# Reordering the first block of a two-branch mixer kernel: when x, u^T's parts and q's scale are made

## The chip, the cores and the metric

One core of a Trainium2 chip runs the whole program. The metric is the device time of one execution, in microseconds (us). The engines are TensorE (PE, its weight loads PEld), VectorE (DVE), ScalarE (ACT), GpSimd (POOL) and the DMA queue that SyncE (SP) issues. Each engine works through its own list of instructions in order.

## The reference, cut to what matters

```python
def reference(x, norm_g, w_in, ...):            # x: 4096 frames x 1024
    u = rms_norm(h, norm_g[layer])
    p = u @ w_in[layer]                          # 1024 x 4616
    (sb_q, sb_k, sb_v, sb_z, m_q, m_k, m_v, m_o, m_z, m_i, m_f) = jnp.split(p, split_at, axis=-1)
    sb = stick_breaking_attention(sb_heads(sb_q), sb_heads(sb_k), sb_heads(sb_v))
    sb_out = sb * jax.nn.silu(sb_z)
    ...
    mix = jnp.concatenate([sb_out, ml_out], axis=-1)
    h = h + mix @ w_out[layer]
    return rms_norm(h, final_norm_g)
```

The change lies in the first block of 512 frames, before any attention: x is normalised to u, u is transposed, and the first projections (v, then q and k) are made from it.

## The kernel before, in words

The frames are worked in blocks of 512 (four tiles p of 128 frames). Each block takes a row of "quanta": a quantum is one product of the transposed u of the block with 128 columns of weights, 24 matmuls of 128x512 (`t_quantum`, L486): for each of eight slices k of the model dimension three passes, high part of the weight times high part of u, high times low, low times high. Weights and u are split into two 16-bit parts each: the high part is a copy by ACT, the low part the difference, by DVE or POOL.

The first block has to make all of this before its first quantum. For each tile p: `x_in(p)` loads 128 rows of x (SP); `u_stats(p)` squares and sums them on ACT (L398) and forms the root on POOL (L400, L401); `u_scale(p)` multiplies them on DVE (L405); `u_first(p)` transposes them on PE (L1389) and copies the two halves out of PSUM, one by DVE (L1393) and one by ACT (L1391), into an fp32 tile; `v_mm(p)` is v's product in fp32 from that tile (L1406, called here the p-th fp32 product, from 0); `v_fin(p)` writes v's two parts (L583, L584) and the gates (L588) with v's scale. `u_parts(p, engine)` makes the 16-bit parts of u^T (ACT copy and subtraction, both at L1397 and L1398) and stores them to DRAM for the later sweeps (`scr_u`, L476).

A weight (`Prep`) is handled in three steps. `top` finds the largest absolute value (two reductions L279, then L282, L284, L286 on DVE). `scale` turns it into a scale by one PE transpose (L290) and five small DVE instructions (L292 to L297; the last writes `wgs`). `split` multiplies each of the two raw pieces by the scale (L307), takes the high part by ACT (L302) and the low part by subtraction (L303). The raw pieces of q (pair 0) lie in tiles named ATh, those of k in ATl, of the second q in bP, of the second k in sA. The DVE list of v's scale ends with L1421.

The order of all that is written out by hand at the end of `main_pass`. Things that belong to a later quantum are registered with `at(g, phase, ...)` and issued by `run(g, phase)`: the first q is quantum 2, then k, the second q, the second k. For the second block (tiles 4 to 7), x is loaded, scaled and transposed in the quanta of the first (`u_T`, L469 to L471); from tile 8 on x is loaded by `x_grid`, four transfers of small pieces (L424), and its squares are summed by L432. The pool of x tiles, `st`, has six buffers. `sb_alloc` and `sb_zero` clear the k tiles `kl` and `kh` of the attention.

The diff's lines of the kernel, with the callers:

Of the kernel before, what the change touches and what calls it, by code (L numbers as in the profile page):

```python
# [200 lines left out]
def main_pass(ctx, tc, x2, norm_g, win, win_k, b_ig, b_fg, conv_w, conv_b, hn_g, wout_k, fn_g,  # L201
              out2, scr_u, scr_m, scr_w, scr_M, scr_E, flag):
    nc = tc.nc
    V, G, A, PE, SP = nc.vector, nc.gpsimd, nc.scalar, nc.tensor, nc.sync
# [22 lines left out]
    def at(g, phase=None, fn=None):  # L227
        if phase is None:
            g, phase = g
        acts[g, phase].append(fn)  # L230

    def run(g, phase):
        for fn in acts.pop((g, phase), []):
            fn()
# [30 lines left out]
    class Prep:  # L265
# [31 lines left out]
            V.tensor_scalar(out=self.gs, in0=CT[:, 64:72], scalar1=SC[:, self.sid, 0:1], scalar2=None, op0=ALU.mult)  # L297

        def split(self, engines):
            for (r, k0, h, l), e in zip(self.pieces, engines):  # L300
                self.mult(r, k0, e)
                A.activation(out=h, in_=r, func=AF.Copy)  # L302
                e.tensor_tensor(out=l, in0=r, in1=h, op=ALU.subtract)  # L303

# [82 lines left out]
    def x_in(p):  # L387
        t = us[p] = stage()
        SP.dma_start(out=t, in_=x2[p * 128:(p + 1) * 128, :])
# [3 lines left out]
    def u_stats(p):  # L393
        t = us[p]
        ss = rnorm[p] = sm.tile([128, 1], F32, tag="ss", name="ss")
        ss2 = sm.tile([128, 2], F32, tag="ss2", name="ss2")
        for half in range(2):
            A.activation(out=ph_tile("yx", [128, 512]), in_=t[:, half * 512:(half + 1) * 512], func=AF.Square, scale=DM ** -0.5 / SU,  # L398
                         accum_out=ss2[:, half:half + 1])
        G.tensor_scalar(out=ss, in0=ss2[:, 0:1], scalar1=ss2[:, 1:2], scalar2=EPS / SU ** 2, op0=ALU.add, op1=ALU.add)  # L400
        G.tensor_tensor(out=ss, in0=ss, in1=mhalf[:, 0:1], op=ALU.pow)  # L401
# [106 lines left out]
    kl = [None, None]  # L508
# [4 lines left out]
    def sb_alloc():  # L513
        nonlocal qs, kh
        qs = wp.tile([128, 4, 512], F16, tag="wnb", name="qs")
        kh = wp.tile([128, 4, 640], F16, tag="kh", name="kh")
        for i in range(2):
            kl[i] = ph_tile(f"kl{i}", [128, 2, 640], F16)
            V.memset(kl[i][64:128, 0, :], 0.0)
            V.memset(kl[i][0:64, 1, :], 0.0)  # L520

    def sb_zero(pair):
        V.memset(kh[:, 2 * pair:2 * pair + 2, 0:128], 0.0)
        V.memset(kl[pair][:, :, 0:128], 0.0)

    def sb_scales(s):

# [434 lines left out]
    for p in range(4, 128 + 4):  # L962
        Q, i = divmod(p, 4)
        gq = blk_g(Q - 1)
        if p < NT:
            if Q == 1:
                at(gq + i, "pre", lambda p=p: x_in(p))
                at(gq + 1 + i, "pre", lambda p=p: (u_stats(p), u_scale(p)))
                gu = gq + i + 3
                at(gu, "pre", lambda p=p: u_T(p, 0))  # L970
                at(gu, "mid", lambda p=p: u_T(p, 1))
                at(gu, "post", lambda p=p: u_store(p))
            else:
                gu = gq + 2 * i
                at(gu - 7, "pre", lambda p=p: x_grid(p))
                at(gu - 5, "mid", lambda p=p: grid_stats(p))
                at(gu - 3, "pre", lambda p=p: grid_sum(p))
                at(gu - 2, "mid", lambda p=p: grid_scale(p))
                at(gu - 1, "pre", lambda p=p: grid_T(p))
                at(gu + 1, "pre", lambda p=p: u_split(p, V if p % 2 else G))  # L980
        elif p < 128:
            at(gq + 1 + i, "pre", lambda p=p: u_load(p))
# [365 lines left out]
    with tc.manual_schedule():  # L1348
# [27 lines left out]
        def wfill(name, tag):  # L1376
            return w_first(WTS[0, name], WT[0, name], sb_cols(0)[name], tag)
# [3 lines left out]
        def u_first(p):  # L1381
            t, u = us.pop(p), u_of(p)
            u32[p] = wt_tile().rearrange("p a k t -> p (a k t)").bitcast(F32).rearrange("p (k t) -> p k t", k=KT)
            for half in range(2):
                ks = slice(4 * half, 4 * half + 4)
                ps = ps_tile("zu", [128, 4, 128])
                for k in range(4):
                    c = (4 * half + k) * 128
                    PE.transpose(ps[:, k, :], t[:, c:c + 128], idf)  # L1389
                if half:  # L1390
                    A.activation(out=u32[p][:, ks, :], in_=ps, func=AF.Copy)  # L1391
                else:
                    V.tensor_copy(out=u32[p][:, ks, :], in_=ps)  # L1393

        def u_parts(p, eng):
            u = u_of(p)
            A.activation(out=u[:, 0], in_=u32[p], func=AF.Copy)  # L1397
            eng.tensor_tensor(out=u[:, 1], in0=u32[p], in1=u[:, 0], op=ALU.subtract)  # L1398
            u_store(p)
# [3 lines left out]
        def v_mm(p, tag):  # L1403
            ps = vps[p] = ps_tile(tag, [128, 512])
            for k in range(KT):
                PE.matmul(ps[:, 0:264], u32[p][:, k, :], vraw[:, k, :], start=(k == 0), stop=(k == KT - 1))  # L1406

        def v_fin(p):
            fin_v(0, p, vps.pop(p), SV[:, 0:1], 1.0 / SU)

        def v_top():
            m = sm.tile([128, 24], F32, tag="wm", name="wm")
            V.tensor_reduce(out=m[:, 0:KT], in_=vraw, op=ALU.max, axis=AX.X, apply_absolute_value=True)
            mx = sm.tile([128, 1], F32, tag="wx", name="wx")
            V.tensor_reduce(out=mx, in_=m[:, 0:KT], op=ALU.max, axis=AX.X)
            pv.mb = sm.tile([128, 128], F32, tag="wmb", name="wmb")
            V.tensor_copy(out=pv.mb, in_=mx[:, 0:1].to_broadcast([128, 128]))

        def v_scale():
            pv.scale()  # L1420
            V.tensor_scalar(out=SV, in0=SC[:, WNS[0], 0:1], scalar1=S_QKV, scalar2=None, op0=ALU.mult)  # L1421
# [13 lines left out]
        x_in(2)  # L1435
        x_in(3)
        qk = [wfill("q0", "ATh"), wfill("k0", "ATl"), wfill("q1", "bP"), wfill("k1", "sA")]
        u_stats(1)
        u_scale(1)
        v_mm(0, "pj")  # L1440
        u_stats(2)
        u_first(1)
        u_scale(2)
        v_top()
        v_mm(1, "pj")
        u_stats(3)
        u_first(2)
        u_scale(3)
        v_scale()
        v_mm(2, "o")  # L1450
        v_fin(0)
        u_first(3)
        qk[0].top()
        v_fin(1)
        u_parts(0, G)
        u_parts(1, G)
        run(0, "pre")
        v_mm(3, "o")
        run(0, "mid")
        run(0, "post")  # L1460
        qk[0].scale()
        qk[0].split([V, V])
        v_fin(2)
        u_parts(2, V)
        u_parts(3, G)
        qk[1].top()
        v_fin(3)
        run(1, "pre")
        run(1, "mid")
        run(1, "post")  # L1470
        sb_alloc()
        sb_zero(0)
        sb_zero(1)
        SP.dma_start(out=crow[0:32, 1, :], in_=conv_w[0].rearrange("t (g p) -> (t g) p", p=128))
        SP.dma_start(out=crow[32:40, 1, :], in_=conv_b[0].rearrange("(g p) -> g p", p=128))
        SP.dma_start(out=crow[0:4, 2, :], in_=hn_g[0].rearrange("(g p) -> g p", p=128))
# [112 lines left out]
```

## Time and profile before

| what | value |
|---|---|
| median of three runs | 2234.07 us (2233.28 to 2237.25) |
| the profiled execution | 2233.29 us, its span 2231.4 us |
| busy share of the span | PE 97%, DVE 66%, ACT 47%, POOL 43% |
| mean granted clock of PE | 0.989 of full speed |

The profiled execution spends 1.9 us outside its span. PE is busy nearly all the time after the first 140 us; the idle time that it has lies mostly ahead of that, where tiles, weights and scales of the first block are being made. A row of the timeline gives the start, the duration, the engine, the line, the instruction with its output and inputs, and in square brackets how long the engine stood idle before it and what released it.

### The profile page before, as it was taken

To read this page: it belongs to the slowest core of one execution; us is meant where nothing else is said; L and a number is where in the kernel's file an instruction comes from. 1 tells how busy PE (TensorE), PEld (TensorE's weight loads), DVE (VectorE), ACT (ScalarE), POOL (GpSimd) and SP (SyncE) were. 2 spreads that over 40 slices of the span, in tenths; PEclk is the share of its full clock that TensorE was granted. 3 is DMA by queue.
4 is the path that set the end of the run, shared out by engine and by line. 5 is a ranking of instruction groups with operands and counts; after the bars stand their busy time and mean duration, and the time that the engine had idled before them with its cause. 6 is when DMAs were issued, how large, how long until landed. Compare 5 with 4: busy or idle time off the path is not lost.

```text
span 2231.4 us, 36361 instructions
## 1 busy us (share of the span) xinstructions
PE 2156.6 (97%) x13731; PEld 1374.2 (62%) x13731; DVE 1474.8 (66%) x2886; ACT 1055.5 (47%) x1875; POOL 950.7 (43%) x1296
## 2 busy tenths in 40 slices
PE   6789999999999999999999999999999999999998
PEld 4456665666666666567666667766666666644443
DVE  5777777756777777755555555655555645788885
ACT  3566666555666666543322233333344322545443
POOL 2477777664555555521111011310333210577763
PEclk8899999999999999999999999999999999999999
DMA  6444444221222112222222213333322321555552
GB/s 184 96 80 99 99 98 100 72 72 57 66 74 76 63 63 72 72 85 46 69 76 76 68 61 81 105 113 95 91 71 82 89 75 56 166 175 174 175 178 92
DMA packets 230240, 208.68 MB, mean 94 GB/s; under 512 B 109492, under 2 KB 185320, under 8 KB 230056
## 3 DMA queue, kind: packets, MB, share of 16 engines
q1 hardware_dynamic: 230040, 206.27, 32.3%
q8 instruction: 110, 1.80, 0.3%
q14 instruction: 74, 0.61, 0.1%
q10 hardware_dynamic: 16, 0.00, 0.0%
HBM read 148.43 MB, written 53.61 MB: 91 GB/s over the span
## 4 chain that ended last, share of the span: by engine, by line
PE 80%; DVE 9%; POOL 4%; issue 3%; DMA 2%; ACT 1%; SPq 0%; DVEq 0%; POOLq 0%; ACTq 0%
PE ps_pj L486 34%; PE ps_pj L498 22%; PE ps_pj L1252 7%; PE ps_o L1252 3%; PE ps_at L628 2%; PE ps_zu L1252 2%; PE ps_o L644 2%; DVE zml L455 2%; DMA st<-in_x_dram 1%; PE ps_zu L834 1%; PE ps_zu L877 1%; PE ps_zu L878 1%; PE ps_zu L597 1%; PE ps_zu L596 1%; DVE qs L564 1%
## 5 line engine op out<-in xcount | busy, mean ns | idle before, releaser
L486 PE MATMUL ps_pj<-U,wT 128*128 128x512 f16 x4608 | 1046.4, 382 | 13.9 <-ACT U L1397 7.7
L486 PEld LDWEIGHTS <-wT 128*128 128x128 f16 x4608 | 452.1, 98 | 512.9 <-issue 14.6
L498 PEld LDWEIGHTS <-U 128*128 128x128 f16 x4512 | 441.1, 98 | 58.0 <-DVE kl L576 1.9
L498 PE MATMUL ps_pj<-wna,U 128*128 128x256 f16 (+1 forms) x2976 | 345.0, 273 | 1.9 <-DVE kl L576 1.6
L611 DVE TENSOR_TENSOR_SCAN bP<-bP,D 128x512 f32<-128x512 f32 x128 | 165.4, 1292 | 106.2 <-POOL bP L603 105.5
L1252 PEld LDWEIGHTS <-U 128*128 128x128 f16 x1344 | 131.6, 99 | 155.5 <-issue 1.3
L612 POOL TENSOR_TENSOR sA<-sA,bP 128x510 f32<-128x510 f32 x128 | 141.8, 1108 | 180.3 <-DVE bP L611 176.7
L890 POOL TENSOR_SCALAR rs<-mv 128x4 f32<-128x4 f32 x32 | 7.7, 240 | 453.3 <-DVE kl L784 395.5
L498 PE MATMUL ps_pj<-wnb,U 128*128 128x256 f16 x1536 | 178.1, 273 | 0.0
L785 ACT ACTIVATE kl<-ps_pj,SC 128x512 f32<-128x512 f32 x64 | 44.0, 688 | 232.8 <-PE ps_pj L486 190.6
L836 DVE TENSOR_TENSOR bP<-ps_zu,bP 128x512 f32<-128x512 f32 x32 | 22.1, 692 | 175.2 <-PE ps_at L835 174.2
L821 POOL TENSOR_SCALAR_AFFINE_SELECT bP<-bP 128x512 f32<-128x512 f32 x32 | 24.7, 771 | 255.8 <-DVE bP L820 225.8
L789 DVE SCALAR_TENSOR_TENSOR z<-kl,CT,z 128x512 f32<-128x512 f32 x144 | 115.1, 799 | 20.8 <-ACT z L786 16.0
L1252 PE MATMUL ps_pj<-wT,U 128*128 128x512 f16 x576 | 127.4, 379 | 1.2 <-DVE st L1257 1.2
L1263 ACT ACTIVATE kl<-st 128x512 f32<-128x512 f32 x64 | 40.4, 632 | 167.5 <-DVE st L1257 89.5
L798 ACT ACTIVATE v<-ps_pj,SC 128x256 f32<-128x256 f32 x64 | 30.4, 475 | 156.9 <-PE ps_pj L498 156.3
L633 DVE SCALAR_TENSOR_TENSOR ATl<-ps_at,ATh 128x512 f16<-128x512 f32 (+1 forms) x128 | 87.6, 685 | 16.7 <-ACT ATh L632 14.8
L1244 POOL TENSOR_TENSOR U<-sA,U 128x512 f16<-128x512 f32 x56 | 76.2, 1383 | 49.2 <-ACT U L1240 49.2
L547 ACT ACTIVATE zml<-ps_pj,SC 128x512 f32<-128x512 f32 x32 | 22.0, 688 | 151.1 <-DMA scr_m<-zml 137.5
L644 PE MATMUL ps_o<-ATl,v 128*128 128x256 f16 (+1 forms) x312 | 72.1, 252 | 20.0 <-DVE ATl L633 16.8
L600 ACT ACTIVATE bP<-ps_zu,SX 128x512 f32<-128x512 f32 x128 | 87.8, 686 | 3.6 <-issue 2.0
L601 ACT ACTIVATE sA<-ps_zu,SX 128x512 f32<-128x512 f32 x128 | 88.4, 690 | 0.0
(298 smaller groups left out, 3873.1 us busy)
## 6 DMA issues: line engine op xcount, KB each, us to landing
U<-scr_u SPq DMA_DIRECT2D x96, 512.0 KB
st<-in_x_dram SPq DMA_DIRECT2D x40, 512.0 KB
scr_u<-U SPq DMA_DIRECT2D x32, 512.0 KB
out_dram<-st SPq DMA_DIRECT2D x31, 512.0 KB
st<-in_w_in_dram SPq DMA_DIRECT2D x28, 512.0 KB
st<-in_x_dram SPq DMA_DIRECT2D x96, 128.0 KB
scr_m<-z SPq DMA_DIRECT2D x32, 256.0 KB
bP<-scr_M SPq DMA_DIRECT2D x32, 256.0 KB
```

The source lines that it names most:

```text
L455: V.tensor_scalar(out=z[:, :, b, :], in0=t[:, :, 2 * h + b, :], scalar1=r4[:, 2 * h + b:2 * h + b + 1], scalar2=None, op0=ALU.mult)
L486: PE.matmul(p3, wt[:, a, k, :], u[:, :, b, k, :], start=(k == 0 and i == 0), stop=(k == KT - 1 and i == 2))
L498: PE.matmul(ps[:, c0:c0 + n], u[:, a, k, :], w[:, b, k, 0:n], start=first and j == 0, stop=last and j == len(order) - 1)
L600: A.activation(out=b, in_=z, func=AF.Sigmoid, scale=SX[:, s, pair, 1:2])
L601: A.activation(out=sg, in_=z, func=AF.Sigmoid, scale=SX[:, s, pair, 0:1])
L611: V.tensor_tensor_scan(out=bf, data0=bf, data1=D1[:, ::-1], initial=1.0, op0=ALU.mult, op1=ALU.max)
L612: G.tensor_tensor(out=sg[:, :, 0:255], in0=sg[:, :, 0:255], in1=b[:, :, 1:256], op=ALU.mult)
L633: V.scalar_tensor_tensor(out=l[:, i:, :], in0=ps[:, i:, :], scalar=S_A, in1=h[:, i:, :], op0=ALU.mult, op1=ALU.subtract)
L644: PE.matmul(o[:, q0:q0 + 128 * n], vt[p][:, head, :], t, start=first, stop=False, skip_group_check=True)
L789: V.scalar_tensor_tensor(out=y, in0=raw[:, t:t + 512], scalar=CT[:, 8 * t + grp:8 * t + grp + 1], in1=y, op0=ALU.mult, op1=ALU.add)
L1244: (V if o in (0, 2, 6) else G).tensor_tensor(out=mo[p][:, o, 1], in0=mt[p][o], in1=mo[p][:, o, 0], op=ALU.subtract)
L1252: PE.matmul(ps, a[:, l, k, :], r[:, k, :], start=first and k == 0 and i == 0, stop=last and k == 3 and i == 2, skip_group_check=True)
```

## The change

The change moves calls in the hand-written order and moves eight clears from one engine to another. Nothing is computed differently.

- `split` becomes "multiply both pieces, then make both pairs of parts" (`parts`), and for the first q the three steps are issued apart: `top` behind the scaling of tile 2, `scale` directly behind v's scale, the two multiplications behind `u_parts(2)` and ahead of the last transposes of u, `parts` behind the last fp32 product.
- `u_parts(0)`, `u_parts(1)`, `u_parts(2)` stand behind the copies of their own tile or nearly so, all three subtractions on POOL; `u_parts(3)` goes to DVE. Before, tiles 0, 1 and 3 were POOL's and tile 2 was DVE's, all after the last copies.
- The loads of x for tiles 4 and 5 are issued directly behind the first weights; tiles 6 and 7 move up by one quantum.
- `v_top` stands ahead of the copies of tile 1, `v_fin(0)` and `v_fin(1)` behind the copies of tile 3.
- The clears of `kl` and `kh` go from DVE, between the scalings of tiles 4 and 5, to POOL, ahead of the root of tile 3.

```diff
         def split(self, engines):
-            for (r, k0, h, l), e in zip(self.pieces, engines):
+            for (r, k0, _, _), e in zip(self.pieces, engines):
                 self.mult(r, k0, e)
+            self.parts(engines)
+
+        def parts(self, engines):
+            for (r, _, h, l), e in zip(self.pieces, engines):
                 A.activation(out=h, in_=r, func=AF.Copy)
                 e.tensor_tensor(out=l, in0=r, in1=h, op=ALU.subtract)
...
-            V.memset(kl[i][64:128, 0, :], 0.0)
-            V.memset(kl[i][0:64, 1, :], 0.0)
-
-    def sb_zero(pair):
-        V.memset(kh[:, 2 * pair:2 * pair + 2, 0:128], 0.0)
-        V.memset(kl[pair][:, :, 0:128], 0.0)
+            G.memset(kl[i][64:128, 0, :], 0.0)
+            G.memset(kl[i][0:64, 1, :], 0.0)
+
+    def sb_zero(pair, e=V):
+        e.memset(kh[:, 2 * pair:2 * pair + 2, 0:128], 0.0)
+        e.memset(kl[pair][:, :, 0:128], 0.0)
...
-                at(gq + i, "pre", lambda p=p: x_in(p))
+                at(gq + max(i - 1, 0), "pre", lambda p=p: x_in(p))
...
         qk = [wfill("q0", "ATh"), wfill("k0", "ATl"), wfill("q1", "bP"), wfill("k1", "sA")]
+        run(0, "pre")
         u_stats(1)
         u_scale(1)
         v_mm(0, "pj")
         u_stats(2)
+        sb_alloc()
+        sb_zero(0, G)
+        sb_zero(1, G)
+        v_top()
         u_first(1)
         u_scale(2)
-        v_top()
+        qk[0].top()
         v_mm(1, "pj")
         u_stats(3)
+        u_parts(0, G)
         u_first(2)
         u_scale(3)
         v_scale()
+        qk[0].scale()
+        u_parts(1, G)
+        u_parts(2, G)
+        for r, k0, _, _ in qk[0].pieces:
+            qk[0].mult(r, k0, V)
         v_mm(2, "o")
+        u_first(3)
         v_fin(0)
-        u_first(3)
-        qk[0].top()
         v_fin(1)
-        u_parts(0, G)
-        u_parts(1, G)
-        run(0, "pre")
         v_mm(3, "o")
+        qk[0].parts([V, V])
+        u_parts(3, V)
+        v_fin(2)
+        qk[1].top()
         run(0, "mid")
         run(0, "post")
-        qk[0].scale()
-        qk[0].split([V, V])
-        v_fin(2)
-        u_parts(2, V)
-        u_parts(3, G)
-        qk[1].top()
         v_fin(3)
         run(1, "pre")
         run(1, "mid")
         run(1, "post")
-        sb_alloc()
-        sb_zero(0)
-        sb_zero(1)
```

The lists of three engines show the moves. First DVE before, from q's scale on (wx, SC and wgs are the scale, ATh the raw q, wT its parts, U the parts of u^T):

```order
L292 TENSOR_REDUCE wx<-ps_zu 128x1
L293 TENSOR_SCALAR wx<-wx 128x1
L294 RECIPROCAL SC<-wx 128x1
L295 TENSOR_SCALAR SC<-wx 128x1
L297 TENSOR_SCALAR wgs<-CT,SC 128x8
L307 TENSOR_TENSOR ATh<-ATh,wgs 128x512
L303 TENSOR_TENSOR wT<-ATh,wT 128x512
L307 TENSOR_TENSOR ATh<-ATh,wgs 128x512
L303 TENSOR_TENSOR wT<-ATh,wT 128x512
L584 SCALAR_TENSOR_TENSOR v<-ps_o,SV,v 128x4x64
L588 TENSOR_SCALAR GR<-ps_o 128x8
L1398 TENSOR_TENSOR U<-wT,U 128x1024
```

And DVE of the change, from the same instruction on (here L311 is the multiplication, L307 the subtraction, L1397 the copy of u^T, L588 and L592 are v's parts and gates):

```order
L292 TENSOR_REDUCE wx<-ps_zu 128x1
L293 TENSOR_SCALAR wx<-wx 128x1
L294 RECIPROCAL SC<-wx 128x1
L295 TENSOR_SCALAR SC<-wx 128x1
L297 TENSOR_SCALAR wgs<-CT,SC 128x8
L311 TENSOR_TENSOR ATh<-ATh,wgs 128x512 x2
L1397 COPY wT<-ps_zu 128x512
L588 SCALAR_TENSOR_TENSOR v<-ps_pj,SV,v 128x4x64
L592 TENSOR_SCALAR GR<-ps_pj 128x8
L588 SCALAR_TENSOR_TENSOR v<-ps_pj,SV,v 128x4x64
L592 TENSOR_SCALAR GR<-ps_pj 128x8
L307 TENSOR_TENSOR wT<-ATh,wT 128x512 x2
```

Before, the last copy of u^T and v's first two ends stood above the first of these rows; now q's scale and both of its multiplications stand ahead of the copy that the last fp32 product reads.

POOL before, from the root of tile 3 on (ss is the root):

```order
L400 TENSOR_SCALAR ss<-ss_254 128x1
L401 TENSOR_TENSOR ss<-ss,mhalf 128x1
L1398 TENSOR_TENSOR U<-wT,U 128x1024 x3
L400 TENSOR_SCALAR ss<-ss_378 128x1
L401 TENSOR_TENSOR ss<-ss,mhalf 128x1
```

And POOL of the change, from the first clear to the same place:

```order
L523 MEMSET kl_230 64x640
L524 MEMSET kl_230 64x640
L523 MEMSET kl_233 64x640
L524 MEMSET kl_233 64x640
L527 MEMSET kh 128x2x128
L528 MEMSET kl_230 128x2x128
L527 MEMSET kh 128x2x128
L528 MEMSET kl_233 128x2x128
L404 TENSOR_SCALAR ss<-ss_278 128x1
L405 TENSOR_TENSOR ss<-ss,mhalf 128x1
L1402 TENSOR_TENSOR U<-wT,U 128x1024 x3
```

The eight clears stand ahead of tile 3's root; the three subtractions stay in the same place of POOL's list, now for tiles 0, 1 and 2.

SP's queue before, from the last of the first weights on (scr_u is the store of u^T's parts):

```order
L361 DMA sA<-in_w_in_dram 128x4x128 x2
L476 DMA scr_u<-U 128x2048 x2
L389 DMA st<-in_x_dram 128x1024
L476 DMA scr_u<-U 128x2048 x2
L389 DMA st<-in_x_dram 128x1024
L424 DMA st<-in_x_dram 32x32x32 x4
```

And SP's queue of the change from the same place:

```order
L365 DMA sA<-in_w_in_dram 128x4x128 x2
L393 DMA st<-in_x_dram 128x1024 x2
L480 DMA scr_u<-U 128x2048 x4
L393 DMA st<-in_x_dram 128x1024
L428 DMA st<-in_x_dram 32x32x32 x4
```

The loads of tiles 4 and 5 no longer stand behind stores that wait for POOL's and DVE's subtractions; the load of tile 6 and the four small-piece transfers of tile 8 now stand behind all four stores.

## Rows read from the trace of the kernel before

**Rows 1.** Windows of the span: busy time by engine, PE clock, DMA share, GB/s.

```profile
20.00:30.00 10.00, 9.41 (x50) 7.83 (x49) 5.70 (x19) 3.93 (x6) 1.49 (x1) 1.00 0.01 2
30.00:40.00 10.00, 1.35 (x5) 0.55 (x5) 7.52 (x15) 5.11 (x10) 4.26 (x3) 0.72 0.48 177
...
60.00:70.00 10.00, 4.01 (x17) 1.89 (x16) 7.48 (x18) 5.46 (x15) 3.90 (x6) 0.75 0.46 102
```

**Rows 2.** Timeline of PE from 25 to 73 us.

```profile
26.83 3.83 PE L1406 MATMUL ps_o<-vraw,wT 128*128 128x264 f32 x16 [0.35 <-DVE wT L1393]
...
40.73 4.44 PE L486 MATMUL ps_pj<-U,wT 128*128 128x512 f16 x11 [1.71 <-DVE wm L282]
...
45.11 2.75 PE L486 MATMUL ps_pj<-U,wT 128*128 128x512 f16 x12
...
52.86 5.30 PE L486 MATMUL ps_pj<-U,wT 128*128 128x512 f16 x12 [4.56 <-ACT wT L302]
```

**Rows 3.** Chain of waits from 28 to 62 us: start, duration, what.

```profile
31.53 1.22 DVE wgs L297
...
38.45 2.23 POOL U L1398
...
41.08 6.05 DMA st<-in_x_dram
...
47.24 0.73 ACT yx L398 x2
...
49.81 0.75 DVE st L405
...
51.45 0.70 DVE ATl L307
```

**Rows 4.** Timeline of DVE in the first 60 us.

```profile
15.99 0.69 DVE L1393 COPY wT<-ps_zu 128x512 f32<-128x512 f32 x1 [3.00 <-PE ps_zu L1389]
...
17.26 2.34 DVE L1413 TENSOR_REDUCE wm<-vraw 128x8 f32<-128x2112 f32 x1
...
23.01 0.23 DVE L297 TENSOR_SCALAR wgs<-CT,SC 128x8 f32<-128x8 f32 x1
...
26.08 0.69 DVE L1393 COPY wT<-ps_zu 128x512 f32<-128x512 f32 x1 [1.69 <-PE ps_zu L1389]
...
54.83 0.69 DVE L303 TENSOR_TENSOR wT<-ATl,wT 128x512 f16<-128x512 f32 x1 [0.70 <-ACT wT L302]
```

**Rows 5.** Timeline of ACT from 16 to 50 us.

```profile
21.47 0.60 ACT L1391 ACTIVATE wT<-ps_zu 128x512 f32<-128x512 f32 x1 [3.08 <-PE ps_zu L1389]
...
27.37 2.00 ACT L1397 ACTIVATE U<-wT 128x1024 f16<-128x1024 f32 x2
```

**Rows 6.** Timeline of POOL in the first 45 us.

```profile
1.36 0.53 POOL L1365 MEMSET D<- 128x512 f32 x1
...
18.49 0.30 POOL L400 TENSOR_SCALAR ss<-ss 128x1 f32<-128x1 f32 x1 [4.69 <-ACT yx L398]
...
28.51 4.21 POOL L1398 TENSOR_TENSOR U<-wT,U 128x1024 f16<-128x1024 f32 x2 [9.07 <-ACT U L1397]
```

**Rows 7.** Timeline of DVE and POOL from 127.5 to 135 us.

```profile
128.07 5.92 DVE L455 TENSOR_SCALAR zml<-st,r 128x256 f32<-128x256 f32 x4
...
129.55 4.29 POOL L1497 TENSOR_TENSOR wna<-vraw,wna 128x2112 f16<-128x2112 f32 x1
```

**Rows 8.** Timeline of SP's queue and ACT: small-piece loads of x and their readers.

```profile
41.60 5.42 SPq L424 DMA_DIRECT2D st<-in_x_dram  x4
...
59.24 0.41 ACT L432 ACTIVATE yx<-st 128x256 f32<-128x256 f32 x1
...
122.65 3.17 SPq L424 DMA_DIRECT2D st<-in_x_dram  x4
...
128.90 0.42 ACT L432 ACTIVATE yx<-st 128x256 f32<-128x256 f32 x1 [0.85 <-DMA st<-in_x_dram]
```

**Rows 9.** Waits of PE over the whole span: total us, times, longest.

```profile
PE ps_o L644 <- DVE ATl L633: 16.8, 12, 6.0
```

## Prediction

> **What bounds the kernel now.** I read the windows first, to see where PE is short of work. In the first block it is: between 30 and 40 us it is busy 1.35 of 10 us, between 60 and 70 us 4.01 [rows 1]. The timeline of PE shows what those holes are. q's quantum runs from its second matmul at 40.73, k's starts at 52.86 after 4.56 us of idle [rows 2]. Both holes are waits for DVE and ACT, so the next view is the chain of waits. Read it downwards: q's `wgs` at 31.53, the last of u^T's subtractions at 38.45 on POOL, then a load of x issued at 41.08 and landed 6.05 us later, its squares on ACT at 47.24, its scaling on DVE at 49.81, and behind that scaling, in DVE's list, k's multiplication at 51.45 [rows 3]. So k's weights wait for a load of x that k does not need, and that load waited in SP's queue behind stores of u^T that waited for POOL. From 51.45 on the chain goes on through DVE, ACT, POOL and PE; no transfer that is issued earlier comes into it, so what is gained at 51.45 should reach the end, unless the shift changes who collides with whom.
>
> I therefore follow one instruction, k's first multiplication (51.45 before), and then what its parts hold up, the multiplication of the second q.
>
> **Part 1: the loads of tiles 4 and 5.** They now stand behind the first weights. Between 20 and 30 us the DMA engines do nothing (share 0.01) [rows 1], and tile 5's load took 6.05 us even behind the stores [rows 3]; so both land well before 30 us, and ACT comes to them only after 33 (part 4). The 6.05 us leave the path. What ends the wait next is ACT's own list.
>
> **Part 2: `v_top` and the clears.** DVE stood idle 3.00 us ahead of the copy at 15.99; `v_top`, whose reduction takes 2.34 us, moves into that hole, and q's `top`, which is shorter, takes its old place at 17.26 [rows 4]. Both cost nothing there. The clears go to POOL, into its 4.69 us of idle ahead of 18.49, when tile 3's squares are ready. A POOL clear of 512 elements took 0.53 us; four of 640 and four of 256 come to about 4 us by that row (an estimate), which just fits [rows 6]. No row has a POOL clear beside DVE work: one DVE copy (`wmb`) or scaling could wait for one clear, so 0 to 0.7 us; I take 0, since the copies that PE waits for read PSUM.
>
> The Trainium skill, page "SBUF — State Buffer", section "Who interferes with whom", says that a GpSimd instruction that only writes SBUF holds up a DVE instruction in a two-port mode, but not one with two SBUF inputs. By it the clears could delay `wmb` and one scaling by the bound above, and nothing else; no run here shows it yet.
>
> **Part 3: u^T's parts and q's scale meet on one pair of ports.** ACT makes the high parts of tiles 1 and 2 directly behind the copy at 21.47, about 1.05 us each; a POOL subtraction starts 1.1 us after its ACT copy starts and takes 2.1 us [rows 5, 6]. So POOL subtracts from 23.1 to 25.2 and from 25.2 to 27.4. DVE ends v's scale as before (`wgs` at 23.01 [rows 4]) and comes with q's `wgs` at about 24.0. There I must choose. Before, this very instruction took 1.22 us instead of 0.23, ending when POOL's subtraction of 28.51 plus 4.21 ended [rows 3, 4, 6]: it was blocked. So in the change it waits until 25.2. Then come q's two multiplications, while POOL's next subtraction is already waiting. The nearest rows for that are from a later stage: four scalings of 256 elements on DVE took 5.92 us together [rows 7], though one of 1024 elements takes 0.75 [rows 3]; POOL's instruction of 129.55, which came while the third ran, went ahead of the fourth and held it to the end [rows 7]. So the turn goes to who waited first, and the multiplications start at 27.4 and end at 28.7 (0.69 each, overlapping a little). Only behind them stands the copy that the last fp32 product needs: 28.6 instead of 26.08 [rows 4].
>
> The same section of the Trainium skill says that the pair is an exclusive lock and that issue order decides who blocks; it speaks against this change, since it puts POOL's long instructions beside DVE's multiplications. By it the sum is the one below; without a lock it would be the first rival's.
>
> From there: the last fp32 product starts 0.75 us after its copy and takes 3.83 us [rows 2, 4], so 29.4 to 33.2. Meanwhile DVE does v's first two ends, q's two subtractions and tile 3's subtraction: by 0.69 us for 512 elements [rows 4] I estimate 0.5, 0.5, 0.7, 0.7 and 1.2 us, done by 33. q's quantum starts at 33.2 rather than 40.73, and if the clock stays up it takes twice 2.75 us, not 4.44 and 2.75 [rows 2]: end 38.7.
>
> **Part 4: to k's first multiplication.** ACT's list behind v's last end (33.2 to 33.6) holds the squares of tile 4, from 33.6, and of tile 5, from 35.1 (1.46 us for a tile, twice 0.73). From squares to scaling took 49.81 − 47.24 = 2.57 us, from scaling to k's multiplication 51.45 − 49.81 = 1.64 us [rows 3]. So 35.1 + 2.57 + 1.64 = 39.3 instead of 51.45: 12.1 us earlier. The clears, had they stayed on DVE, would lie on this stretch; now nothing does.
>
> **Part 5: both multiplications first.** For k's two pieces on DVE the old order took 54.83 + 0.69 − 51.45 = 4.07 us, with DVE waiting for ACT 0.70 us twice [rows 3, 4]. In the new order the second multiplication fills the first such wait and the second ACT copy runs under the first subtraction: about 1.35 us for the two multiplications, which overlap a little, and 1.3 for the two subtractions, 2.65 us: 1.4 us saved. For pieces split over POOL and DVE each engine's list is as before: nothing.
>
> **Sum.** 12.1 + 1.4 = 13.5 us at the second q's multiplication. Behind it DVE's chain (second k, z) is as before and PE still has a hole there [rows 1], so the shift is kept whole. The profiled 2233.3 − 13.5 = 2219.8; the median of the runs lies 0.8 us above the profiled time, so 2220.5. PE's granted clock is the main unknown of size: 12 matmuls took 5.30 us at the lower level and 2.75 at the higher [rows 2], and where its falls lie against the work shifts; I allow 2 us either way.
>
> **Rivals.**
> - *No collision on POOL's ports.* If DVE gets its multiplications in between, or the subtractions come late enough, the last copy stays at about 26.7. Part 4 then gives 37.1, the sum is 15.8 us: 2218.3. For it: what was blocked before was a single instruction with no POOL work queued behind the subtraction [rows 3, 6]. Against it: rows 7.
> - *Tile 8's small pieces come late.* Its transfers now stand behind all four stores, so they are issued near 34 instead of 41.60. ACT wants them 59.24 − 51.45 = 7.8 us after k's multiplication, less the 1.4 of part 5, so at 45.7, with everything for the second q behind them. In the quiet case they were there 128.90 − 122.65 = 6.25 us after issue: 40, no wait. In the busy case the rows say only that they were there when ACT came, 59.24 − 41.60 = 17.6 us after issue: 51.6 [rows 3, 8]. At that end 5.9 us of the gain go: 2226.4. Against it: tiles 4 and 5 no longer share the DMA engines with them.
> - *The gain is given back later.* PE has a 6.0 us wait for DVE's ATl near 137 [rows 9], made by the port collision of rows 7. If something not moved set that stage, all would be absorbed there: 2234. Against it: the chain between runs through compute that is shifted too. The collision may also come out shorter, up to 4 us, which would go below 2217.
> - *Slower.* The clears on POOL stand ahead of tile 3's root and so of its scaling on DVE, its transposes and the last product. They have 4.69 us of idle [rows 6], and the root has about 2.2 us more, since the scaling that needs it stands near 21.6, 1.4 us ahead of v's `wgs` [rows 4]. They eat the whole gain when the eight take over 6.9 + 13.5 = 20.4 us, 2.5 us each; at 3.3 us each the time is 2240. Against it: 0.53 us for 512 elements; even POOL's slowest row per element (4.29 us for 2112, 2 ns) makes under 8 us of them [rows 6, 7].
>
> **How the numbers follow.** Forecast 0.50 (its own range 2218.5 to 2222.5), no collision 0.22, late small pieces 0.14 (2223 to 2227), given back 0.09, slower 0.05. The range 2215 to 2226.5 holds the first two and most of the third. A change of under 0.2% (4.5 us) is about what a measurement of this kernel can't tell from none. Faster by more is the first three and a part of the fourth: 0.87; same 0.08; slower 0.05.
>
> **What would show it.** Right: tiles 4 and 5's squares start on ACT without a wait for a transfer; q's `wgs` on DVE stretched to over 1 us, its multiplications behind POOL's third subtraction, the last copy at 28 to 29; q's quantum from about 33, k's from about 40.7; the second q's some 13.5 us earlier, with PE idle ahead of it as now; the hole near 137 found again some 13 us earlier, at much the same length. Wrong: ACT waiting for a load between 33 and 46; the clears ending after 19 or holding DVE; the later hole longer by what was gained.

## The result, and the profile after

The kernel after takes 2221.91 us (median of 6 runs, 2220.13 to 2222.97) and the kernel before 2234.1 us (median of 6, 2233.28 to 2238.92): a ratio of 0.9941, 95% interval 0.993 to 0.9951, or 12.2 us less. The prediction was 2220.5 us, range 2215 to 2226.5. The profiled execution took 2221.8 us, with a span of 2220.0 us and a mean granted clock of 0.990.

The windows of the kernel after, in the columns of [rows 1]:

```profile
20.00:30.00 10.00, 7.37 (x42) 6.05 (x40) 8.11 (x18) 5.24 (x9) 6.83 (x4) 1.00 0.43 174
30.00:40.00 10.00, 9.55 (x45) 5.95 (x45) 8.17 (x24) 4.86 (x12) 1.79 (x4) 1.00 0.65 166
```

Between 30 and 40 us PE is busy 9.55 of 10 us, where it was 1.35 [rows 1]. The DMA engines work between 20 and 30 us (0.43 instead of 0.01), since the stores of u^T come earlier.

The timeline of PE, after, which answers to [rows 2] and to the wait of [rows 9]:

```profile
10.47 6.11 PE L1410 MATMUL ps_pj<-vraw,wT 128*128 128x264 f32 x16 [0.77 <-DVE wT L1397]
...
17.80 3.83 PE L1410 MATMUL ps_pj<-vraw,wT 128*128 128x264 f32 x16 [0.35 <-DVE wT L1397]
...
30.18 3.83 PE L1410 MATMUL ps_o<-vraw,wT 128*128 128x264 f32 x16 [2.57 <-DVE wT L1397]
33.84 2.75 PE L490 MATMUL ps_pj<-U,wT 128*128 128x512 f16 x12
...
41.62 4.74 PE L490 MATMUL ps_pj<-U,wT 128*128 128x512 f16 x12 [1.89 <-ACT wT L306]
...
55.49 0.44 PE L290 MATMUL ps_zu<-idf,wmb 128*128 128x128 f32 x1 [5.55 <-DVE wmb L286]
...
124.62 0.27 PE L648 MATMUL ps_o<-ATl,v 128*128 128x128 f16 x1 [5.99 <-DVE ATl L637]
```

q's quantum starts at 33.84 instead of 40.73 and keeps the higher clock, k's starts at 41.62 instead of 52.86. The last fp32 product pays for it: it waits 2.57 us for its copy, where it waited 0.35 [rows 2]. Ahead of the second q's quantum PE still stands idle for 5.55 us.

The timeline of DVE, after, which answers to [rows 4]:

```profile
16.03 0.41 DVE L1421 COPY wmb<-wx 128x128 f32<-128x128 f32 x1
17.05 0.69 DVE L1397 COPY wT<-ps_zu 128x512 f32<-128x512 f32 x1 [0.61 <-PE ps_zu L1393]
17.66 0.94 DVE L409 TENSOR_SCALAR st<-st,ss 128x1024 f32<-128x1024 f32 x1
...
24.98 1.34 DVE L297 TENSOR_SCALAR wgs<-CT,SC 128x8 f32<-128x8 f32 x1
26.35 3.17 DVE L311 TENSOR_TENSOR ATh<-ATh,wgs 128x512 f32<-128x512 f32 x2
29.45 0.68 DVE L1397 COPY wT<-ps_zu 128x512 f32<-128x512 f32 x1
...
38.58 0.75 DVE L409 TENSOR_SCALAR st<-st,ss 128x1024 f32<-128x1024 f32 x1 [0.85 <-POOL ss L405]
...
49.05 0.69 DVE L311 TENSOR_TENSOR bP<-bP,wgs 128x512 f32<-128x512 f32 x1
```

The timeline of POOL, after, which answers to [rows 6]:

```profile
14.41 0.63 POOL L523 MEMSET kl<- 64x640 f16 x1
...
17.75 0.30 POOL L528 MEMSET kl<- 128x256 f16 x1
19.55 0.30 POOL L404 TENSOR_SCALAR ss<-ss 128x1 f32<-128x1 f32 x1 [1.50 <-ACT yx L402]
...
20.48 2.14 POOL L1402 TENSOR_TENSOR U<-wT,U 128x1024 f16<-128x1024 f32 x1
24.16 4.21 POOL L1402 TENSOR_TENSOR U<-wT,U 128x1024 f16<-128x1024 f32 x2 [1.54 <-ACT U L1401]
```

Read the two side by side. POOL subtracts without a break from 24.16 to 28.37. DVE's `wgs`, 0.23 us when alone [rows 4], comes in that stretch and takes 1.34; the two multiplications behind it take 3.17 us (the first alone 2.57: it waits until POOL's last subtraction has ended), and the copy that PE waits for is pushed to 29.45. The eight clears run from 14.41 to 18.05, and POOL then still waits 1.50 us for the squares of tile 3, so in this execution they hold nothing up on POOL.

The chain of waits of the kernel after, where [rows 3] had a load of x:

```profile
35.96 0.73 ACT yx L402 x2
...
38.58 0.75 DVE st L409
...
40.21 0.70 DVE ATl L311
```

The transfer is gone: the chain now goes through the squares of tile 5 on ACT, the root on POOL, the scaling, and k's multiplication at 40.21 instead of 51.45.

### The profile page after: what moved, and what is told of

Its sections match the earlier page's. It is cut to its first block, busy times and chain, and to the rows that moved or that the text cites. A ratio compares the mean times of both kernels' runs of the same rounds, so it can differ in the third digit from the quotient of the medians.

```text
span 2220.0 us, 36362 instructions
## 1 busy us (share of the span) xinstructions
PE 2155.0 (97%) x13731; PEld 1373.9 (62%) x13731; DVE 1471.9 (66%) x2878; ACT 1054.1 (47%) x1875; POOL 953.4 (43%) x1304
## 4 chain that ended last, share of the span: by engine, by line
PE 80%; DVE 8%; POOL 5%; issue 3%; DMA 1%; ACT 1%; SPq 0%; DVEq 0%; POOLq 0%; ACTq 0%
PE ps_pj L490 34%; PE ps_pj L502 22%; PE ps_pj L1256 7%; PE ps_o L1256 3%; PE ps_at L632 2%; PE ps_zu L1256 2%; PE ps_o L648 2%; DVE zml L459 2%; PE ps_zu L838 1%; PE ps_zu L881 1%; PE ps_zu L882 1%; PE ps_zu L601 1%; PE ps_zu L600 1%; DMA st<-in_x_dram 1%; DVE qs L568 1%
## 5 line engine op out<-in xcount | busy, mean ns | idle before, releaser
L648 PE MATMUL ps_o<-ATl,v 128*128 128x256 f16 (+1 forms) x312 | 72.1, 252 | 20.1 <-DVE ATl L637 16.9
## 6 DMA issues: line engine op xcount, KB each, us to landing
st<-in_x_dram SPq DMA_DIRECT2D x96, 128.0 KB, 4.4
```

The costliest lines, as they stand in the source:

```text
L648: PE.matmul(o[:, q0:q0 + 128 * n], vt[p][:, head, :], t, start=first, stop=False, skip_group_check=True)
```

## The experiments

**What is compared.** Executions differ by when the first fp32 product starts and what it takes (5.51 us before, 6.11 after; more on that at the end), so marks are counted from the start of the second fp32 product: 16.73 before, 17.80 after. Two marks are used: k's first multiplication on DVE, at 51.45 − 16.73 = 34.72 before and 40.21 − 17.80 = 22.41 after, and the multiplication of the second q (bP), at 44.93 before and 31.25 after. By the second mark the change gains 13.68 us. A third, the end of PE's 6 us wait near 137 (120.29 before, 106.82 after: 13.47), turned out to be a poor one (last experiment). The rows of the kernel before that these marks need and that are not shown yet, from the timelines of PE and DVE:

```profile
16.73 3.83 PE L1406 MATMUL ps_pj<-vraw,wT 128*128 128x264 f32 x16 [0.35 <-DVE wT L1393]
...
61.66 0.69 DVE L307 TENSOR_TENSOR bP<-bP,wgs 128x512 f32<-128x512 f32 x1
```

| kernel | median us | ratio to before, 95% | k's multiplication | bP |
|---|---|---|---|---|
| before | 2234.1 | 1 | 34.72 | 44.93 |
| after | 2221.91 | 0.9941 (0.993 to 0.9951) | 22.41 | 31.25 |
| loads only | 2229.23 | 0.9972 (0.9962 to 0.9982) | 29.97 | 40.18 |
| all but the loads | 2224.05 | 0.9949 (0.9933 to 0.9966) | 24.69 | 33.92 |
| clears on DVE | 2222.18 | 0.9939 (0.9923 to 0.9956) | 23.67 | 33.45 |
| old split | 2223.47 | 0.9951 (0.9933 to 0.9969) | 22.42 | 32.62 |
| multiplications behind the copy | 2218.68 | 0.9934 (0.9918 to 0.9949) | 20.54 | 29.36 |
| third subtraction late | 2219.98 | 0.9944 (0.9929 to 0.9959) | 22.03 | 30.86 |
| squares early | 2218.46 | 0.993 (0.9916 to 0.9944) | 20.61 | 29.43 |
| three together | 2219.93 | 0.9936 (0.9922 to 0.995) | 20.41 | 29.23 |

Each ratio is to the kernel before on the same chip in the same batch. Medians of different batches are not compared finer than that: the second four ran beside a median of 2233.82 us for the kernel before, the first four beside 2235.15.

The theory is that of the prediction: the loads, u^T's parts and the clears each held k's multiplication, and a collision of DVE and POOL gives part of it back. The rival is that one part alone, the loads, brings the gain, and that the collision is without effect.

**1. The loads alone** (edit to the kernel before):

```diff
-                at(gq + i, "pre", lambda p=p: x_in(p))
+                at(gq + max(i - 1, 0), "pre", lambda p=p: x_in(p))
         qk = [wfill("q0", "ATh"), ...]
+        run(0, "pre")
...
         u_parts(1, G)
-        run(0, "pre")
```

> The kernel before with one part of the change alone: the loads of tiles 4 and 5 behind the first weights (6 and 7 one quantum up). Marker for all runs: the matmul that ends PE's 6.0 us wait for ATl, 137.02 us in the trace before, 124.62 in the trace of the change. My theory (loads, early parts and scale, and the order of the two multiplications each hold a share): k's multiplication no longer waits for x and follows DVE's and ACT's own lists, about 46.5 instead of 51.45, so the marker comes 5.0 us earlier, 132.0, and the time is near 2229. Rival (the loads are the whole gain, the rest is hidden behind them): marker near 124.6, time near 2222.

k's multiplication came 4.75 us earlier than before. The timeline of DVE in this run shows what holds it now:

```profile
43.22 0.75 DVE L405 TENSOR_SCALAR st<-st,ss 128x1024 f32<-128x1024 f32 x1
44.10 0.33 DVE L519 MEMSET kl<- 64x320 uint32 x1
...
46.13 0.17 DVE L524 MEMSET kl<- 128x128 uint32 x1
46.22 0.62 DVE L405 TENSOR_SCALAR st<-st,ss 128x1024 f32<-128x1024 f32 x1
47.21 0.29 DVE L292 TENSOR_REDUCE wx<-ps_zu 128x1 f32<-128x128 f32 x1 [0.36 <-PE ps_zu L290]
```

With the transfer gone, DVE's list is full: the clears, two scalings, k's scale. Only the last 0.36 us are a wait, for PE's transpose of k's scale. The rival, that the loads alone bring the gain, falls: 4.75 us of 13.68.

**2. All but the loads** (edit to the kernel after):

```diff
-                at(gq + max(i - 1, 0), "pre", lambda p=p: x_in(p))
+                at(gq + i, "pre", lambda p=p: x_in(p))
         qk = [wfill("q0", "ATh"), ...]
-        run(0, "pre")
...
         u_parts(1, G)
+        run(0, "pre")
         u_parts(2, G)
```

> The change without its loads: tile 4's load again behind the stores of tiles 0 and 1, tile 5's behind those of tiles 2 and 3. My theory: tile 5's load is issued near 34 and lands 4 to 6 us later, so its squares start at 38 to 40 instead of 35.96, k's multiplication at 42.3 to 44.3 instead of 40.21; marker 126.7 to 128.7, time 2224 to 2226. Rival (the loads are the whole gain): marker back near 137, time near 2234.

The timeline of ACT in this run has the wait for the transfer again:

```profile
37.59 0.63 ACT L402 ACTIVATE yx<-st 128x512 f32<-128x512 f32 x1 [2.41 <-DMA st<-in_x_dram]
```

k's multiplication comes 2.28 us later than after, about that wait. bP comes 2.67 later; the 0.39 more is k's first half quantum, longer at the lower clock (5.13 us instead of 4.74). So this side alone gains 11.01 us at bP, and the loads alone 4.75: together 15.8, though the change gains 13.7. The two parts hide 2.1 us of each other, and a share of the gain can't be given to either without naming what is done already.

**3. The clears back on DVE** (edit to the kernel after):

```diff
-            G.memset(kl[i][64:128, 0, :], 0.0)
-            G.memset(kl[i][0:64, 1, :], 0.0)
+            V.memset(kl[i][64:128, 0, :], 0.0)
+            V.memset(kl[i][0:64, 1, :], 0.0)
...
-        sb_alloc()
-        sb_zero(0, G)
-        sb_zero(1, G)
         v_top()
...
         run(1, "post")
+        sb_alloc()
+        sb_zero(0)
+        sb_zero(1)
```

> The change with the eight clears back on DVE, between the scalings of tiles 4 and 5. My theory: they took 2.2 us there, DVE waits 0.85 us for tile 5's root in the trace of the change, so tile 5's scaling and k's multiplication come 1.3 us later; marker 125.9, time near 2223. Rival (a clear costs nothing on either engine): marker 124.6. If the clears held up DVE from POOL by more than they cost on DVE, the marker would be earlier than 124.6.

k's multiplication is 1.26 us late (1.3 expected), bP 2.20: behind the later start k's first half quantum and the four transposes behind it met the lower clock longer (5.30 us instead of 4.74, and 1.03 instead of 0.60). The median, 2222.18, does not show it: the intervals of the two ratios overlap almost wholly.

**4. The old order of `split`** (edit to the kernel after):

```diff
-            for (r, k0, _, _), e in zip(self.pieces, engines):
+            for (r, k0, h, l), e in zip(self.pieces, engines):
                 self.mult(r, k0, e)
-            self.parts(engines)
+                A.activation(out=h, in_=r, func=AF.Copy)
+                e.tensor_tensor(out=l, in0=r, in1=h, op=ALU.subtract)
```

> The change with the old order inside split (multiply, copy, subtract, piece by piece), which concerns k alone, since q's steps are issued apart and the others are split over POOL and DVE. My theory: k's parts end 1.4 us later; marker 126.0, time near 2223.3. Rival (ACT's squares of tile 8, not k's parts, set the second q's start, so the order of the multiplications is hidden): marker 124.6.

k's first multiplication stays (22.42 against 22.41), and bP comes 1.37 us late: the term of part 5 (1.4 expected).

**5. q's multiplications behind the last copy** (edit to the kernel after), to take the copy out of the collision:

```diff
-        for r, k0, _, _ in qk[0].pieces:
-            qk[0].mult(r, k0, V)
         v_mm(2, "o")
         u_first(3)
+        for r, k0, _, _ in qk[0].pieces:
+            qk[0].mult(r, k0, V)
         v_fin(0)
```

> The change with q's two multiplications behind the last copy of u^T on DVE instead of ahead of it. Times are counted from the start of the second fp32 product, since the first one's length varies with PE's granted clock from run to run: in the trace of the change k's first multiplication stands at 22.41, the end of PE's 6.0 us wait at 106.82. My theory (the multiplications, held by POOL's third subtraction, hold the copy and with it the last product, whose end sets the squares of tiles 4 and 5): the last product starts 2.3 us earlier, k's multiplication at 20.4, the wait's end near 104.8, time 2220. Rival (the last product is not what k waits for): 22.4 and 106.8, time as with the change, 2221.9.

The timeline of DVE in this run:

```profile
27.06 0.69 DVE L1397 COPY wT<-ps_zu 128x512 f32<-128x512 f32 x1 [0.89 <-PE ps_zu L1393]
27.67 1.71 DVE L311 TENSOR_TENSOR ATh<-ATh,wgs 128x512 f32<-128x512 f32 x2
```

The copy waits for PE alone, and the last fp32 product starts 10.16 us behind the second (27.81 − 17.65) instead of 12.38. k's multiplication comes 1.87 us earlier than after (expected 2.0). That is the price of holding the copy; the first rival had put it at 2.3 us (15.8 less 13.5). The collision of `wgs` itself stays (1.34 us again). The multiplications still take 1.71 us instead of 1.29, since POOL's last subtraction is running when they come, but nothing urgent stands behind them.

**6. The third subtraction of u^T late** (edit to the kernel after), so that POOL has nothing queued when DVE multiplies:

```diff
         u_parts(1, G)
-        u_parts(2, G)
         for r, k0, _, _ in qk[0].pieces:
             qk[0].mult(r, k0, V)
...
         v_fin(1)
+        u_parts(2, G)
```

> The change with u_parts(2) behind v_fin(1), so that POOL's third subtraction starts only after q's multiplications: the collision itself taken away, DVE's order kept. My theory: the two multiplications take 1.3 us together instead of 3.17, the last product starts 1.8 us earlier, but ACT's copy for tile 2 now stands ahead of q's high parts, so k's multiplication gains 1.4 us: 21.0 from the second product's start. Rival (DVE's multiplications are slow for another reason than POOL's instruction): they still take about 3.2 us and nothing moves.

The timelines of DVE and PE in this run:

```profile
24.08 1.34 DVE L297 TENSOR_SCALAR wgs<-CT,SC 128x8 f32<-128x8 f32 x1
25.46 1.29 DVE L311 TENSOR_TENSOR ATh<-ATh,wgs 128x512 f32<-128x512 f32 x2
26.67 0.68 DVE L1397 COPY wT<-ps_zu 128x512 f32<-128x512 f32 x1
...
29.57 2.81 DVE L307 TENSOR_TENSOR wT<-ATh,wT 128x512 f16<-128x512 f32 x2 [0.80 <-ACT wT L306]
32.31 1.21 DVE L1402 TENSOR_TENSOR U<-wT,U 128x1024 f16<-128x1024 f32 x1
...
27.41 3.83 PE L1410 MATMUL ps_o<-vraw,wT 128*128 128x264 f32 x16 [0.69 <-DVE wT L1397]
```

With POOL's queue empty the same two multiplications take 1.29 us, not 3.17, and `wgs` still 1.34 behind the subtraction that runs. The last fp32 product starts 10.51 us behind the second (27.41 − 16.90) instead of 12.38 (12.59 in both repeats of the kernel after, run 9). That is the collision shown by itself. But k gained only 0.38 us, not the 1.4 expected: the subtraction put off collided again, with q's two subtractions (2.81 us instead of 1.27), and tile 3's subtraction behind these held q's quantum to 33.57, 2.12 us of idle. The squares did come earlier, and k then followed DVE's own list, which these subtractions had made longer, and a wait of 0.34 us for the transpose of its scale. A collision moved is not a collision removed.

**7. The squares of tiles 4 and 5 early on ACT** (edit to the kernel after):

```diff
-                at(gq + 1 + i, "pre", lambda p=p: (u_stats(p), u_scale(p)))
+                at(gq + 1 + i, "pre", lambda p=p: (p > 5 and u_stats(p), u_scale(p)))
...
         u_parts(2, G)
+        u_stats(4)
+        u_stats(5)
```

> The change with the squares of tiles 4 and 5 on ACT directly behind u_parts(2), ahead of the last product, where ACT stands idle 2.6 us; their scalings keep their place on DVE. My theory: DVE no longer waits for the roots (0.80 and 0.85 us in the trace of the change), k's multiplication comes 1.6 us earlier, at 20.8; DVE's own list then sets it, and moving the last product would no longer help. Rival (DVE's list is what k waits for already): 22.4.

k's multiplication comes 1.80 us earlier than after (1.6 expected), with the collision unchanged (3.18 us). The timeline of DVE in this run:

```profile
36.65 1.41 DVE L409 TENSOR_SCALAR st<-st,ss 128x1024 f32<-128x1024 f32 x2
```

The two scalings stand back to back, without the 0.80 and 0.85 us of waiting for POOL's roots. So part 4's list on ACT was indeed what set k after the change.

**8. Three together**: 5, 7, and tile 3's subtraction on POOL (`u_parts(3, G)` instead of `u_parts(3, V)`).

> Multiplications behind the copy, squares of tiles 4 and 5 early, and the subtraction of tile 3 on POOL instead of DVE, which takes 1.2 us off DVE's list. My theory: k's multiplication 3.3 us earlier than with the change, at 19.1; behind it q's quantum becomes the limit for k's start (q starts no earlier than POOL's subtraction allows, about 33.8 in the clock of the trace of the change), so the second q gains about 3: time near 2219. Rival (the holes left on PE and the phases of its clock take it back): same as the change within 1 us.

Missed: 20.41 instead of 19.1. The timelines of PE and DVE in this run:

```profile
34.98 2.53 PE L490 MATMUL ps_pj<-U,wT 128*128 128x512 f16 x11 [2.55 <-POOL U L1402]
...
33.79 1.16 DVE L282 TENSOR_TENSOR wm<-wm,CT 128x8 f32<-128x8 f32 x1
...
37.66 0.29 DVE L292 TENSOR_REDUCE wx<-ps_zu 128x1 f32<-128x128 f32 x1 [0.47 <-PE ps_zu L290]
```

Tile 3's subtraction on POOL came so late that q's quantum waited 2.55 us for it, and the transpose of k's scale stands in PE's list behind half of that quantum. What was saved on DVE was lost there. DVE's own list comes only 0.47 us ahead of that transpose: a small step of k's `top` (L282), 0.17 us in the kernel after, took 1.16 beside that subtraction. The collision had moved once more, and without the wait for PE some 0.8 of the 1.3 us would still be missing (an estimate, 1.31 less 0.47).

**9. Both kernels again, unchanged**, two profiled executions of each:

> The kernel before, unchanged, to see how much of a profiled execution's time belongs to that execution. If the start of the second fp32 product (16.73 before, 17.80 after) hangs on the execution and not on the change, the four repeats of the two kernels spread over 16.7 to 18.4 us with no order by kernel; if the change itself delays it, both of before stay at 16.7 within 0.2 us. From that start to the end of PE's 6 us wait for DVE it should take 120.3 us again, within 0.3 us.

> The kernel after, unchanged. If the start hangs on the execution, as for the repeat of before; if on the change, 17.8 within 0.2 us again. From that start to the end of PE's 6 us wait 106.8 us again, within 0.3 us. At PE's 2.33 us hole near 1947 us: if the fall of the granted clock behind it belongs to the change, it comes again; if to the execution, it can be missing, and the time is then some 1.3 us less.

> As for the first repeat of the kernel before: second fp32 product's start somewhere between 16.7 and 18.4 us if it hangs on the execution, 16.7 if on the kernel; 120.3 us from there to the end of PE's 6 us wait.

> As for the first repeat of the kernel after: start between 16.7 and 18.4 us, or 17.8 if it hangs on the kernel; 106.8 us from there to the end of PE's 6 us wait; the fall of the clock near 1947 us again, if it belongs to the kernel.

The second fp32 product started at 18.24 and 16.75 us in the repeats of before, at 17.61 and 16.95 in those of after: no order by kernel. bP stood at 44.95 and 44.92 behind it before, and at 31.43 and 31.46 after, so this mark holds within 0.2 us, and the gain by it is 13.5 to 13.7 us. k's multiplication stood at 34.74 and 34.72 before, at 22.61 and 22.63 after. Differences of 0.2 us between runs 2 to 8 and the kernel after are therefore not read.

The 0.2 us have a visible source: in both repeats of after the collision takes another form. The timeline of DVE in the first:

```profile
20.29 2.21 DVE L286 COPY wmb<-wx 128x128 f32<-128x128 f32 x1
...
26.79 1.42 DVE L297 TENSOR_SCALAR wgs<-CT,SC 128x8 f32<-128x8 f32 x1
28.25 1.29 DVE L311 TENSOR_TENSOR ATh<-ATh,wgs 128x512 f32<-128x512 f32 x2
29.45 0.68 DVE L1397 COPY wT<-ps_zu 128x512 f32<-128x512 f32 x1
```

In the first profile q's `wmb` started 0.26 us ahead of POOL's first subtraction (20.22 and 20.48) and took 0.23 us. Here it started 0.01 us behind it (20.29 and 20.28), and 0.09 in the second repeat, and took 2.21 and 2.12. From there each of POOL's three subtractions held one step of DVE: `wmb`, v's `wgs` (1.74 and 1.72 us), q's `wgs` (1.42 and 1.41). The multiplications then took 1.29 us without any edit. So 3.17 us is the form of one execution. What all three profiles share is that the multiplications end behind POOL's last subtraction, and that the copy starts at 11.65 to 11.85 us behind the second product.

The third mark does not hold. It was expected again within 0.3 us, and came at 122.07 and 120.86 before (120.29 in the first profile), at 106.57 and 107.21 after. Two lines of PE's timeline in the first repeat of before show what differs:

```profile
128.05 0.55 PE L628 MATMUL ps_at<-idf,sA 128*128 128x128 f32 x3 [2.66 <-POOL sA L612]
...
140.31 0.27 PE L644 MATMUL ps_o<-ATl,v 128*128 128x128 f16 x1 [4.33 <-DVE ATl L633]
```

The same kernel has one hole of 5.99 us in one execution, holes of 2.66 and 4.33 in another. The collision of [rows 7] is the same in both (DVE's four scalings take 5.92 us again); the first hole, a wait for POOL, lies ahead of it. Behind that hole the 24 matmuls up to the second took 6.95 us instead of 5.35, with a granted clock of 0.60 between 128.0 and 132.3, and this shortens the second hole. What brings the first hole stays open. The same pair of waits, 2.66 and 4.33, stands in run 3, which came 4.0 us late by this mark. So what runs 3, 4 and 5 showed there, up to 4 us, can't be read as an effect of their edits, and their verdicts rest on the two earlier marks.

The other question was a loss near 1947 us, where the shift between the first two profiles drops from 12.66 us to 11.39. The timeline of PE in the kernel after, first profile:

```profile
1947.31 0.56 PE L1074 MATMUL ps_zu<-mtop,ones 128*128 128x4 f32 x2 [2.33 <-DVE mtop L1215]
1947.87 9.21 PE L1256 MATMUL ps_pj<-wT,U 128*128 128x512 f16 x36
```

and in its first repeat:

```profile
1947.05 0.36 PE L1074 MATMUL ps_zu<-mtop,ones 128*128 128x4 f32 x2 [2.31 <-DVE mtop L1215]
1947.62 7.93 PE L1256 MATMUL ps_pj<-wT,U 128*128 128x512 f16 x36 [0.21 <-DVE st L1261]
```

The same 36 matmuls behind the same wait took 9.21 and 7.93 us. The granted clock between 1946.9 and 1950.4 us was 0.52 in the first profile and 1.00 in both repeats. The repeats' spans were 2218.4 and 2218.6 us, 1.6 and 1.4 less than the first. That loss belongs to the execution.

## Why the prediction was right

**Part 1 (loads): right.** The squares of tile 4 start on ACT at 34.42 and those of tile 5 at 35.96, neither behind a wait for a transfer. Run 2 shows the price without it.

**Part 2 (clears): right in sign, small error.** Eight POOL clears took 3.6 us against the estimate of 4 (4.2 in both repeats). They held up two DVE instructions, against the value 0 taken from the range 0 to 0.7, so one of the prediction's own signs of being wrong was there: v's `wmb` took 0.41 us instead of 0.23 and a scaling 0.94 instead of 0.75 (1.21 and 1.32 in the repeats), while the copy out of PSUM beside them kept 0.69 and v's reduction 2.35 (2.34 before). By the rule of the Trainium skill that the prediction quoted (page "SBUF — State Buffer", section "Who interferes with whom"), a copy or a scaling between SBUF tiles can be held up so, and the trace agrees. In the first profile the delays did not reach q's path. In the repeats the longer scaling left q's `wmb` behind the start of POOL's first subtraction (run 9), and k's multiplication stands 0.2 us later. In the second repeat the clears held tile 3's root as well: its squares were ready at 17.49 us and the root started at 18.74, with no later effect than in the first (k's multiplication at 22.63 and 22.61). Run 3 prices the clears on DVE at 1.3 us.

**Part 3 (collision): right.** Counted with the later start of 1.07 us, `wgs` ends at 26.32 (25.2 forecast), the multiplications end at 29.52 (28.7), the last product starts at 30.18 (29.4) and q's quantum at 33.84 (33.2): each is 0.6 to 1.1 us late, so the steps between them were right within 0.5 us. Run 6 shows the cause by taking POOL's queued subtraction away. One premise, that v's scale ends as before, held in the first profile only; in the repeats v's `wgs` was held as well. The forecast did not suffer, since POOL's last subtraction sets the end either way. The rival without a collision is not what happens, but run 5 shows that its price was near the mark. The rival's own sum has a slip: from a copy at 26.7 instead of 28.6, 1.9 us earlier, the steps of part 4 give 37.4 and not 37.1.

**Part 4 (k's multiplication): right.** 40.21 against 39.3 forecast, 0.9 us late with a start 1.07 us late; the gain from that start is 34.72 − 22.41 = 12.31 (12.1 forecast; 12.1 in the repeats).

**Part 5 (order of `split`): right.** 1.37 us in run 4 against 1.4.

**The sum.** 12.31 + 1.37 = 13.68 us at bP, against 13.5. The median fell by 12.2 us; its interval, some 11 to 15.6 us, holds both. Between the first two profiles the later start took 1.07 us and the clock near 1947 took 1.27, while 0.26 came between: 13.47 − 1.07 + 0.26 − 1.27 = 11.39, and the spans differ by 11.4. Both losses vary from execution to execution (run 9); the three profiled executions of each kernel average 2234.04 and 2220.82 us, 13.2 apart. The allowance of 2 us for the clock was the right kind of term.

**The rivals.** *Late small pieces*: ACT squares the first of them at 47.34, with no wait for a transfer. *Given back later*: PE's wait for ATl is 5.99 us long in both first profiles, 12.4 us earlier, and its total over the span 16.9 us against 16.8 [rows 9]. *Slower by the clears*: 3.6 us, not 20.4. The bound of under 8 us that the prediction gave them took 2 ns per element for POOL's slowest row; the multiplication by CT near 8 us took 3.02 us for 1056 elements, 2.9 ns, which makes some 10 us of them, still far from 20.4.

**Open.** Why the granted clock comes back sooner within the first fp32 product in one execution of a kernel than in another. How the 11.01 us of run 2 divide between the early parts of u^T and the early scale of q: the runs price only the clears and the order of `split` in them. Nor was a version found that is faster than after beyond doubt: the ratios of runs 5 and 7, 0.9934 and 0.993, lie some 1.6 and 2.5 us below that of the change, 0.9941, but the intervals overlap.

## What to carry to other kernels

Follow one instruction that everything later hangs on, list what stands ahead of it on its engine, and price the parts in their order: each stall removed uncovers the next, and here two parts worth 4.75 and 11.0 us alone were worth 13.7 together. When an early step is put beside another engine's long instructions, write down who waits for the shared port and what is queued behind: a short wait of DVE became 2 us of idle TensorE because a copy stood behind it. Compare traces from a mark that has been seen to hold over repeats, and look at the repeats of a collision too, or what one execution shows is taken for an effect.

## What the runs showed of the hardware that was not expected

One and the same kernel gives up to 1.5 us of difference in where its second fp32 product starts. The first product on PE's timeline, and a window over most of it (PEclk is the third figure from the end), in the first repeat of the kernel before:

```profile
10.30 6.72 PE L1406 MATMUL ps_pj<-vraw,wT 128*128 128x264 f32 x16 [1.30 <-DVE wT L1393]
```

```profile
10.30:15.50 5.20, 5.20 (x12) 4.06 (x13) 0.75 (x1) 2.23 (x7) 3.25 (x5) 0.50 1.13 313
```

and in the second:

```profile
10.28 5.25 PE L1406 MATMUL ps_pj<-vraw,wT 128*128 128x264 f32 x16 [1.28 <-DVE wT L1393]
```

```profile
10.30:15.50 5.20, 5.20 (x18) 4.21 (x19) 0.75 (x1) 2.21 (x7) 3.24 (x5) 0.72 1.13 315
```

Sixteen fp32 matmuls that start within 0.02 us of each other end 1.49 us apart, with a granted clock of 0.50 (1.2 GHz, the lower level) throughout the window in the one and of 0.72 in the mean in the other. In half-microsecond windows the clock is back at 1.00 from 13.5 us in the second repeat and only from 16.5 in the first. At the higher level (2.4 GHz) these matmuls take 3.83 us, as the second product does. Near 1947 us, too, a wait of 2.15 to 2.33 us was followed by a clock of 0.52 in one execution and of 1.00 in two others of the same kernel.

The port collision, too, is decided by little: whether q's `wmb` started 0.26 us ahead of POOL's subtraction or 0.01 us behind it made its time 0.23 or 2.21 us in two executions of the same kernel.
